# Seven block products for two pairs of each mixer's output projection

## The chip, the cores and the metric

The kernel runs on one core of a Trainium2 chip, as one launch. TensorE multiplies, VectorE and ScalarE work elementwise and empty the accumulators, GpSimd does a little, SyncE issues the loads of the weights. The metric is the device time of the launch in microseconds. The kernel before takes 925.27 us (median of three runs, 924.82 to 926.18).

## The reference, cut to what matters

Two decoder layers over 256 rows of 1024 columns, in float32. Each layer adds half a gated feed-forward network, a mixer, and half a second such network, with a norm ahead of each.

```python
def swiglu(x, w_gate, w_up, w_down):
    return (jax.nn.silu(x @ w_gate) * (x @ w_up)) @ w_down

def ab_mixer(x, w_in, v_norm, w_s, b_s, w_out):          # layer 0
    qa, ka, va, ub, vb = jnp.split(x @ w_in, [512, 1024, 1536, 2048], axis=-1)
    a_out = mixture_of_dilations(heads(qa), heads(ka), heads(va))   # 8 heads of 64
    b_out = gelu(ub) * (causal(w_s) @ rms_norm(gelu(vb), v_norm) + b_s)   # 4 groups of 128
    return jnp.concatenate([a_out, b_out], axis=-1) @ w_out

def c_mixer(x, w_in, w_out):                             # layer 1
    q, k, v = jnp.split(x @ w_in, 3, axis=-1)            # 16 heads of 64, causal softmax
    return from_heads(attention(q, k, v)) @ w_out
...
for layer in range(2):
    h = h + 0.5 * swiglu(rms_norm(h, ffn1_norm[layer]), ...)
    h = h + mixer(rms_norm(h, mix_norm[layer]))
    h = h + 0.5 * swiglu(rms_norm(h, ffn2_norm[layer]), ...)
return rms_norm(h, final_norm)
```

This is a summary of the reference with the shapes put in. With 256 rows the first mixer's three dilations become one masked softmax whose mask holds the logarithm of how many patterns reach a key, and the second mixer's block selection becomes plain causal attention.

## The kernel before

**Products in three parts.** Each float32 operand is split into a high and a low part (`split` L241, `Stream.split_piece` L92: ScalarE copies the high part, VectorE subtracts it from the operand), and each product is three matmuls: high by high, high by low, low by high (`mm3` L236, `rowwise` L377, `colwise` L385, `part` L449).

**The weight stream.** `Stream` (L39) holds every weight of the program in the order of use, in chunks of 1 MB: 512 columns by four k tiles, 256 columns by eight, or, for the second matrix of a stage, a pair of k tiles by 1024 columns. Three raw buffers are loaded ahead (SyncE's queue) and four split buffers are in use or ready. `take` hands out the next chunk, `free` gives one back and `pump` (L117) then issues what has become possible: the next load, the next split. So where `free` stands decides when the following chunks are split. `add_cols` has a number of pieces, in how many parts a chunk is split.

**Two ways to project.** `project` (L401) multiplies the transposed result of a stage (`tiles`, k tiles by two row halves) with the second matrix and adds to the residual `xr`. In the plain way (`part`) a pair of k tiles is 2 k x 2 row halves x 2 column halves, three matmuls each. In the other way (`mixed_part` L412) a pair is seen as two by two blocks times two by two blocks and multiplied by seven products in place of eight. The feed-forward stages do this for the pairs in `MIXED`. It needs sums of blocks on both sides: of the rows (`mix_rows`, L715: four VectorE steps on 128 columns, and a split of the 384 new columns into `seh` and `sel`) and of the weights (`split_mixed` L96: four VectorE steps on 512 columns into `wx`, and their split into `wxh` and `wxl`, one buffer of each). The products of all mixed pairs of a stage gather in seven PSUM banks: `(0,0)`, `(0,1)`, `(1,0)`, 1, 5, 6 and 7. After the last one VectorE and ScalarE join them into the residual (L428 to L445); the lower row half's four steps (`second_rows`) come after the statistics of the upper half. The order of products is sums first for an even pair and own blocks first for an odd one.

**The end of a stage.** The last four k tiles of `project` run for the first row half, whose norm is then formed and transposed under the second row half's matmuls. The second row half's norm (`pend[1].turn`) is transposed within the first block of the next stage. In the feed-forward stages and the second mixer this stands ahead of the last k tile of that block, and the two chunks of the last projection are freed behind it (`behind`, L395). In the first mixer it stands in the middle of its second block, and those two chunks are freed at the end of `project` (L530).

**The first mixer** (`ab_mixer` L844): two blocks of V's 512 columns and two of the gate's 512 columns (each block one row half, 24 matmuls of 512 columns), then four column blocks of u, then q and k for eight heads in eight column blocks, then the projection. `keep_g` (L884) puts the gate's rows through gelu, four sums of squares, a power on GpSimd and a scaling into `vn`. `mixing` (L909) multiplies `vn` with the turned spatial weights for one of four groups, adds a bias, multiplies with u and splits.

**The second mixer** (`c_mixer` L960): two blocks of V's first 512 columns, q and k for heads 0 to 7, two blocks of V's second 512 columns, q and k for heads 8 to 15, then the projection.

**Attention** (`make_attention` L758) runs between these: `scores` of four heads at a time, softmax on VectorE, ScalarE and, in the second mixer, GpSimd; `turn` transposes a head's probabilities; `weighted` forms the weighted sums of V for two heads in one bank and `weighted_two` does so for two pairs in two banks, each split into `mix`. A list of events hung on numbered slots (a slot is one column block of 24 matmuls, a half block, or a k tile of the projection) says when each is traced:

```python
for h, s in enumerate((10, 11, 11, 12, 14, 14, 15, 15)):
    at(s, turn, h)
for h, s in enumerate((8, 8, 8, 8, 12, 12, 12, 12)):
    at(s, scores, h)
for p, s in ((0, 13), (2, 16)):
    at(s, weighted, p)
```

The order of instructions on each engine is fixed when the program is built. A planner there gives each engine, among the instructions whose operands its cost model has ready, the one that was traced first; on the chip each engine runs its list in that order. PSUM has eight banks, handed out by `bank()`.

## Time and profile before

| | |
|---|---|
| median of three runs | 925.27 us |
| profiled execution | 924.85 us |
| its span, first to last instruction | 923.1 us |
| TensorE busy | 915.7 us |
| VectorE busy | 691.9 us |
| ScalarE busy | 538.2 us |
| granted TensorE clock | 0.999 |

A line of the profile names the kernel's line, the engine, the operation, the tile written and the tile read. PE is TensorE, PEld its weight loads, DVE VectorE, ACT ScalarE, POOL GpSimd. A line can be that of a helper: L93 and L94 are every split of a weight, L242 and L243 every other split.

### The profile page before, as it was taken

The page shows a single profiled execution, that of the slowest core. Times are in us where ns is not written, and L with a number is a line of the kernel's source. Part 1 is how long each engine was busy: PE and PEld are TensorE (multiplying, and loading weights), DVE is VectorE, ACT ScalarE, POOL GpSimd, SP SyncE. Part 2 cuts the span into 40 slices and gives each one's busy share as a digit, 9 for nine tenths or more (in the row PEclk, how much of TensorE's full clock was granted, in tenths as well). Part 3 has the DMA queues.
Part 4 walks back from the last instruction along what each step waited for, and adds up shares of the span by engine and source line. Part 5 has one row for each costly group of instructions (what it writes and reads, how often), then busy time and mean ns, then how long its engine had stood idle before and what let it go on. Part 6 is the DMA issues. An engine that isn't in the chain of part 4 may idle for free.

```text
span 923.1 us, 15780 instructions
## 1 busy us (share of the span) xinstructions
PE 915.7 (99%) x6442; PEld 843.2 (91%) x6442; DVE 691.9 (75%) x1044; ACT 538.2 (58%) x842; POOL 35.5 (4%) x53
## 2 busy tenths in 40 slices
PE   9999999999999999999999999999999999999997
PEld 8999998889889999988899999888989799999886
DVE  6886779977657566879876678898656575677797
ACT  6754555585867455546664555556756674555552
POOL 0000000000000000000000000000323100000000
PEclk9999999999999999999999999999999999999999
DMA  9885554757526766536486665473744457665351
GB/s 324 270 275 182 186 180 141 270 175 249 167 91 191 221 185 195 192 131 242 153 274 185 195 207 179 162 243 129 250 150 146 129 167 225 203 204 185 137 182 45
DMA packets 125704, 175.79 MB, mean 190 GB/s; under 512 B 3264, under 2 KB 104768, under 8 KB 125632
## 3 DMA queue, kind: packets, MB, share of 16 engines
q1 hardware_dynamic: 123952, 172.60, 57.5%
q10 hardware_dynamic: 1680, 2.19, 0.8%
q8 instruction: 50, 0.82, 0.4%
q14 instruction: 22, 0.18, 0.1%
HBM read 173.73 MB, written 1.05 MB: 189 GB/s over the span
## 4 chain that ended last, share of the span: by engine, by line
PE 99%; issue 1%; DVE 0%; ACT 0%; POOLq 0%; POOL 0%
PE bank L391 18%; PE bank L393 18%; PE bank L392 18%; PE bank L458 5%; PE bank L462 5%; PE bank L459 5%; PE bank L239 4%; PE bank L237 4%; PE bank L238 4%; PE bank L381 3%; PE bank L383 3%; PE bank L382 3%; PE bank L822 1%; PE bank L782 1%; PE bank L342 1%; PE bank L810 1%
## 5 line engine op out<-in xcount | busy, mean ns | idle before, releaser
L93 ACT ACTIVATE whi<-raw 128x1024 fp32r<-128x1024 f32 (+1 forms) x336 | 329.0, 1029 | 238.8 <-PE bank L392 102.8
L94 DVE TENSOR_TENSOR wlo<-raw,whi 128x1024 fp32r<-128x1024 f32 (+1 forms) x336 | 385.1, 1184 | 84.3 <-ACT whi L93 83.7
L391 PE MATMUL bank<-xTh,whi 128*128 128x256 f32 x1440 | 399.7, 278 | 0.0
L393 PE MATMUL bank<-xTh,wlo 128*128 128x256 f32 x1440 | 398.2, 277 | 0.0
L392 PE MATMUL bank<-xTl,whi 128*128 128x256 f32 x1440 | 398.2, 276 | 0.0
L391 PEld LDWEIGHTS bank<-xTh,whi 128*128 128x128 f32 x1440 | 270.3, 188 | 1.3 <-issue 1.2
L392 PEld LDWEIGHTS bank<-xTl,whi 128*128 128x128 f32 x1440 | 270.8, 188 | 0.1
L393 PEld LDWEIGHTS bank<-xTh,wlo 128*128 128x128 f32 x1440 | 270.5, 188 | 0.0
L674 DVE TENSOR_TENSOR hm<-sil,bank 128x512 f32<-128x512 f32 x38 | 26.1, 687 | 57.2 <-PE bank L393 57.1
L458 PE MATMUL bank<-whi,hTh 128*128 128x512 f32 x152 | 59.8, 393 | 0.0
L459 PE MATMUL bank<-wlo,hTh 128*128 128x512 f32 x152 | 59.2, 390 | 0.0
L242 ACT ACTIVATE hTh<-hm 128x512 fp32r<-128x512 f32 x39 | 24.5, 627 | 50.1 <-DVE hm L719 38.9
L462 PE MATMUL bank<-whi,hTl 128*128 128x512 f32 x152 | 51.4, 389 | 0.0
L94 DVE TENSOR_TENSOR wxl<-wx,wxh 128x1536 fp32r<-128x1536 f32 x24 | 42.1, 1755 | 11.3 <-ACT wxh L93 11.2
L381 PE MATMUL bank<-whi,xTh 128*128 128x512 f32 x112 | 44.4, 397 | 0.0
L383 PE MATMUL bank<-whi,xTl 128*128 128x512 f32 x112 | 43.8, 391 | 0.0
L382 PE MATMUL bank<-wlo,xTh 128*128 128x512 f32 x112 | 43.6, 390 | 0.0
L93 ACT ACTIVATE wxh<-wx 128x1536 fp32r<-128x1536 f32 x24 | 35.5, 1481 | 11.6 <-DVE wx L108 7.7
L249 POOL TENSOR_TENSOR rstd<-ms,half_neg 128x1 f32<-128x1 f32 x14 | 8.1, 582 | 797.2 <-DVE ms L283 792.9
L462 PEld LDWEIGHTS bank<-whi,hTl 128*128 128x128 f32 x152 | 28.5, 188 | 6.0
L459 PEld LDWEIGHTS bank<-wlo,hTh 128*128 128x128 f32 x152 | 28.6, 188 | 5.6
L458 PEld LDWEIGHTS bank<-whi,hTh 128*128 128x128 f32 x152 | 28.6, 188 | 5.5
(165 smaller groups left out, 1150.5 us busy)
## 6 DMA issues: line engine op xcount, KB each, us to landing
raw<-in_ffn_w_down SPq DMA_DIRECT2D x44, 1024.0 KB, 5.0
raw<-in_ffn_w_gate SPq DMA_DIRECT2D x38, 1024.0 KB, 5.5
raw<-in_ffn_w_up SPq DMA_DIRECT2D x38, 1024.0 KB, 5.4
raw<-in_c_w_in SPq DMA_DIRECT2D x12, 1024.0 KB, 5.4
raw<-in_ab_w_in SPq DMA_DIRECT2D x10, 1024.0 KB, 5.4
raw<-in_ffn_w_up SPq DMA_DIRECT2D x12, 512.0 KB, 6.5
raw<-in_ffn_w_gate SPq DMA_DIRECT2D x8, 512.0 KB, 4.0
raw<-in_ab_w_out SPq DMA_DIRECT2D x4, 1024.0 KB, 5.0
```

Of the source, the lines that this page charges most:

```text
L93: self.nc.scalar.activation(hi, raw, AF.Copy)
L94: self.nc.vector.tensor_sub(lo, raw, hi.bitcast(F32))
L237: nc.tensor.matmul(p, sh, mh, start=start, stop=False)
L381: nc.tensor.matmul(p, xh, w[0][:, k, :], start=k0 + k == 0, stop=False)
L382: nc.tensor.matmul(p, xh, w[1][:, k, :], start=False, stop=False)
L383: nc.tensor.matmul(p, xl, w[0][:, k, :], start=False, stop=k0 + k == KD - 1)
L391: nc.tensor.matmul(p, h, xh, start=k == 0, stop=False)
L392: nc.tensor.matmul(p, h, xl, start=False, stop=False)
L393: nc.tensor.matmul(p, l, xh, start=False, stop=k == KD - 1)
L458: nc.tensor.matmul(banks[t, h], sh, w[0][:, kw, cs], start=first, stop=False)
L459: nc.tensor.matmul(banks[t, h], sh, w[1][:, kw, cs], start=False, stop=False)
L462: nc.tensor.matmul(banks[t, h], sl, w[0][:, kw, cs], start=False, stop=last)
```

## The change

- In both mixers two of the four pairs of the output projection are mixed: k tiles 4 to 7 in the first (the gating's four groups), 0 to 3 in the second. `mix_rows` moves out of the feed-forward stage. The mixers get a pool `mq` for the mixed rows and for `wx`, `wxh`, `wxl`.
- The first mixer's gate comes first, V's 512 columns come last, ahead of the projection. The second half's norm is turned in the first block ahead of its last k tile, and the two chunks of the last projection are freed behind that; `project` no longer frees them. Its four chunks for the gate and u are split in four pieces.
- In the second mixer V's second 512 columns come after all q and k. The slots of both mixers are renumbered.
- The weighted sums of two pairs go to the two halves of one bank. Where the pair is mixed, ScalarE copies the bank to SBUF, and the mixed rows and the split are made from the copy.
- The first mixer's gating results are kept for two groups together, for the mixed rows.

```diff
@@ -191,24 +191,23 @@
 
     add_ffn(a["ffn1_w_gate"][0], a["ffn1_w_up"][0], a["ffn1_w_down"][0])
     wab = a["ab_w_in"][0]
-    add_cols(wab, 1024, 512)
-    add_cols(wab, 2048, 512)
-    add_cols(wab, 1536, 256)
-    add_cols(wab, 1792, 256)
+    add_cols(wab, 2048, 512, 4)
+    add_cols(wab, 1536, 256, 4)
+    add_cols(wab, 1792, 256, 4)
     for c in range(2):
         add_cols(wab, c * 256, 256)
         add_cols(wab, 512 + c * 256, 256)
-    add_rows(a["ab_w_out"][0], (4, 6, 0, 2))
+    add_cols(wab, 1024, 512)
+    add_rows(a["ab_w_out"][0], (4, 6, 0, 2), (4, 6))
     add_ffn(a["ffn2_w_gate"][0], a["ffn2_w_up"][0], a["ffn2_w_down"][0])
     add_ffn(a["ffn1_w_gate"][1], a["ffn1_w_up"][1], a["ffn1_w_down"][1])
     wc = a["c_w_in"][0]
     add_cols(wc, 2048, 512, 4)
     for c in range(4):
-        if c == 2:
-            add_cols(wc, 2560, 512)
         add_cols(wc, c * 256, 256, 2 if c else 4)
         add_cols(wc, 1024 + c * 256, 256, 2 if c else 4)
-    add_rows(a["c_w_out"][0], (0, 2, 4, 6))
+    add_cols(wc, 2560, 512)
+    add_rows(a["c_w_out"][0], (0, 2, 4, 6), (0, 2))
     add_ffn(a["ffn2_w_gate"][1], a["ffn2_w_up"][1], a["ffn2_w_down"][1])
 
 
@@ -524,12 +523,21 @@
                     if c == 1 and h == 1 and i == 0:
                         n0.turn_half(1)
                 if c == 1:
-                    add = n1.add(h, banks[1, h], factor)
-                    square = n1.square(h)
+                    n1.add(h, banks[1, h], factor)
+                    n1.square(h)
         n1.root()
-        if nxt == 1:
-            behind(square, add, lambda: st.free(2))
-
+
+
+    def mix_rows(pool, k, hm, e):
+        a11, a21, a12, a22 = (hm[:, i * 128 : (i + 1) * 128] for i in range(4))
+        e = e[:, :384].rearrange("p (j c) -> p j c", j=3)
+        nc.vector.tensor_add(e[:, 0, :], a21, a22)
+        nc.vector.tensor_sub(a21, a11, a21)
+        nc.vector.tensor_sub(e[:, 1, :], e[:, 0, :], a11)
+        nc.vector.tensor_sub(e[:, 2, :], a12, e[:, 1, :])
+        parts = [pool.tile([128, 3, 128], F32R, name=f"{n}{k}") for n in ("seh", "sel")]
+        split(*parts, e)
+        return parts
 
     def heat(n):
 
@@ -712,16 +720,6 @@
             def keep(k, hm):
                 split(hT[0][:, k : k + 2], hT[1][:, k : k + 2], hm.rearrange("p (k t c) -> p k t c", k=2, t=NT))
 
-            def mix_rows(k, hm):
...
             if begin:
                 with tc.tile_pool(name="bp", bufs=1) as bp, tc.manual_schedule():
                     hm = begin(bp, fp, pb)
@@ -748,14 +746,14 @@
                         turn_all()
                 hm = gated(*ps2)
                 if k in MIXED:
-                    mix_rows(k, hm)
+                    mixed[k] = mix_rows(mq, k, hm, fp.tile([128, 512], F32, name="sil", bufs=2))
                 keep(k, hm)
 
             turn_all()
             project(hT, [k + j for k in DOWN for j in range(2)], 4, 0.5, phase + 1, mixed=mixed)
 
 
-    def make_attention(mp, mask_cols, nheads, v, mix, engine):
+    def make_attention(mp, mask_cols, nheads, v, mix, engine, mixed={}, seven=()):
         qs, ks, scs, probs, pts = {}, {}, {}, {}, {}
         mask = mp.tile([128, 384], F32, name="mask")
         nc.scalar.dma_start(mask, a["consts"][:, mask_cols])
@@ -812,8 +810,7 @@
                 pts[p] = mp.tile([128, 2, 384], F32, name="pt", bufs=3)
             nc.scalar.copy(pts[p][:, j, :], tp[:, :384])
 
-        def weighted(p):
-            o = bank()
+        def weighted(p, o):
             pt = pts.pop(p)
...
@@ -821,12 +818,20 @@
                     vs = slice(p * 128 + j * 64, p * 128 + j * 64 + 64)
                     last = nc.tensor.matmul(o[r, S - n : S], v[:, t, vs], pt[:, j, c0 : c0 + n],
                                             start=t == 0, stop=t == 1)
-            split(mix[0][:, p], mix[1][:, p], o[:, :S].rearrange("p (t c) -> p t c", t=NT))
             return last
 
         def weighted_two(p):
-            with tc.issue_after(weighted(p + 1).ins):
-                weighted(p)
+            o = bank()
+            with tc.issue_after(weighted(p + 1, o[:, S:]).ins):
+                weighted(p, o[:, :S])
+            if p in seven:
+                hm = mp.tile([128, 512], F32, name="hm", bufs=2)
+                nc.scalar.copy(hm, o)
+                mixed[p] = mix_rows(st.mix_pool, p, hm, mp.tile([128, 512], F32, name="e"))
+                split(mix[0][:, p : p + 2], mix[1][:, p : p + 2], hm.rearrange("p (k t c) -> p k t c", k=2, t=NT))
+                return
+            for q in (p + 1, p):
+                split(mix[0][:, q], mix[1][:, q], o[:, (q - p) * S : (q - p + 1) * S].rearrange("p (t c) -> p t c", t=NT))
 
         return put_q, put_k, scores, turn, weighted_two
 
@@ -842,7 +847,9 @@
 
 
     def ab_mixer(phase):
-        with tc.tile_pool(name="mp", bufs=1) as mp:
+        with tc.tile_pool(name="mp", bufs=1) as mp, tc.tile_pool(name="mq", bufs=1) as mq:
+            st.mix_pool = mq
+            mixed = {}
             mix = mix_tiles(mp)
             v = v_tile(mp, 512)
             vn = mp.tile([128, NT, 512], F32, name="vn")
@@ -866,17 +873,30 @@
                                         base=0, channel_multiplier=-1)
 
             ws, pb = {}, {}
-
-            def block(t, m, mid=None):
+            ev = {}
+            slot = 0
+
+            def at(s, f, *args):
+                ev.setdefault(s, []).append(lambda: f(*args))
+
+            def step():
+                nonlocal slot
+                run_events(ev, slot)
+                slot += 1
+
+            def block(t, m, mid=None, turned=None):
                 pb[t, m] = bank()
                 for i in range(2):
-                    if i == 1 and mid:
-                        mid()
                     if t == 0:
                         ws[m, i] = st.take()
-                    rowwise(pb[t, m], t, i * 4, ws[m, i], range(4))
+                    if i and turned:
+                        rowwise(pb[t, m], t, 4, ws[m, i], range(3))
+                        turned()
+                    rowwise(pb[t, m], t, i * 4, ws[m, i], range(3, 4) if i and turned else range(4))
                     if t == 1:
                         st.free()
+                    if mid:
+                        mid()
 
             def keep_v(t):
                 nc.vector.tensor_copy(v[:, t, :], pb[t, 0])
@@ -897,31 +917,30 @@
                     nc.vector.scalar_tensor_tensor(vn[:, t, cs], g[:, cs], y[:, q : q + 1], vgain[:, cs],
                                                    op0=ALU.mult, op1=ALU.mult)
 
-            block(0, 0)
-            block(0, 1, pend[1].turn)
-            keep_v(0)
+            block(0, 1, turned=lambda: pend[1].turn((nc.vector, nc.scalar)))
+            behind(*pend[1].turned, lambda: st.free(2))
             keep_g(0)
-            block(1, 0)
             block(1, 1)
-            keep_v(1)
             keep_g(1)
+            twos = []
 
             def mixing(g):
                 p = bank()
                 for t in range(NT):
                     nc.tensor.matmul(p[:, t * 128 : (t + 1) * 128], vn[:, t, g * 128 : (g + 1) * 128],
                                      wsT[:, g, :], start=True, stop=True)
-                tmp = mp.tile([128, NT, 128], F32, name="tmp", bufs=2)
+                if g % 2 == 0:
+                    twos.append(mp.tile([128, 512], F32, name="tmp", bufs=2))
+                two = twos[-1]
+                tmp = two[:, g % 2 * S : g % 2 * S + S].rearrange("p (t c) -> p t c", t=NT)
                 pv = p[:, :S].rearrange("p (t c) -> p t c", t=NT)
                 for t in range(NT):
                     nc.vector.tensor_add(tmp[:, t, :], pv[:, t, :], sbias[:, g * 128 : (g + 1) * 128])
                 nc.vector.tensor_mul(tmp, tmp, uT[:, g, :].rearrange("p (t c) -> p t c", t=NT))
-                split(mix[0][:, 4 + g], mix[1][:, 4 + g], tmp)
-
-            ev = {}
-
-            def at(s, f, *args):
-                ev.setdefault(s, []).append(lambda: f(*args))
+                if g % 2:
+                    mixed[3 + g] = mix_rows(mq, 3 + g, two, mp.tile([128, 512], F32, name="e"))
+                    split(mix[0][:, 3 + g : 5 + g], mix[1][:, 3 + g : 5 + g],
+                          two.rearrange("p (k t c) -> p k t c", k=2, t=NT))
 
             turn_spatial()
             for i, s in enumerate((2, 4, 5, 6)):
@@ -930,18 +949,16 @@
                 at(s, turn, h)
             for h, s in enumerate((8, 8, 8, 8, 12, 12, 12, 12)):
                 at(s, scores, h)
-            for p, s in ((0, 13), (2, 16)):
+            for p, s in ((0, 17), (2, 19)):
                 at(s, weighted, p)
 
-            slot = 0
             for c in range(2):
                 w = st.take()
                 for j in range(2):
                     p = bank()
                     colwise(p[:, :S], w, j)
                     nc.scalar.activation(uT[:, 2 * c + j, :], p[:, :S], AF.Gelu_apprx_tanh)
-                    run_events(ev, slot)
-                    slot += 1
+                    step()
                 st.free()
             for c in range(2):
                 for put in (put_q, put_k):
@@ -950,18 +967,23 @@
                         p = bank()
                         colwise(p[:, :S], w, j)
                         put(2 * c + j, p)
-                        run_events(ev, slot)
-                        slot += 1
+                        step()
                     st.free()
-            project(mix, [4, 5, 6, 7, 0, 1, 3, 2], 4, 1.0, phase + 1, lambda i: run_events(ev, 12 + i))
+            for t in range(NT):
+                block(t, 0, step)
+                keep_v(t)
+            project(mix, [4, 5, 6, 7, 0, 1, 3, 2], 4, 1.0, phase + 1, lambda i: step(), mixed)
             assert not ev
 
 
     def c_mixer(phase):
-        with tc.tile_pool(name="mp", bufs=1) as mp:
+        with tc.tile_pool(name="mp", bufs=1) as mp, tc.tile_pool(name="mq", bufs=1) as mq:
+            st.mix_pool = mq
+            mixed = {}
             mix = mix_tiles(mp)
             v = v_tile(mp, D)
-            put_q, put_k, scores, turn, weighted = make_attention(mp, slice(384, 768), 16, v, mix, nc.gpsimd)
+            put_q, put_k, scores, turn, weighted = make_attention(mp, slice(384, 768), 16, v, mix, nc.gpsimd,
+                                                                  mixed, (0, 2))
             ws, pb = {}, {}
 
             def block(t, m, mid=None, turned=None):
@@ -991,20 +1013,17 @@
                 run_events(ev, slot)
                 slot += 1
 
-            for h, s in enumerate((6, 7, 7, 8, 10, 11, 12, 12, 18, 18, 19, 19, 22, 22, 23, 23)):
+            for h, s in enumerate((6, 7, 7, 8, 10, 11, 11, 12, 14, 15, 15, 16, 18, 18, 19, 19)):
                 at(s, turn, h)
-            for h, s in enumerate((4, 4, 4, 4, 8, 8, 8, 8, 16, 16, 16, 16, 20, 20, 20, 20)):
+            for h, s in enumerate((4, 4, 4, 4, 8, 8, 8, 8, 12, 12, 12, 12, 16, 16, 16, 16)):
                 at(s, scores, h)
-            for p, s in ((0, 10), (2, 14), (4, 21), (6, 24)):
+            for p, s in ((0, 10), (2, 14), (4, 21), (6, 23)):
                 at(s, weighted, p)
 
             block(0, 0, turned=lambda: pend[1].turn((nc.vector, nc.scalar)))
             behind(*pend[1].turned, lambda: st.free(2))
             block(1, 0)
             for c in range(4):
-                if c == 2:
-                    block(0, 1, step)
-                    block(1, 1, step)
                 for put in (put_q, put_k):
                     w = st.take()
                     for j in range(2):
@@ -1013,7 +1032,9 @@
                         put(2 * c + j, p)
                         step()
                     st.free()
-            project(mix, [0, 1, 2, 3, 4, 5, 7, 6], 4, 1.0, phase + 1, lambda i: step())
+            block(0, 1, step)
+            block(1, 1, step)
+            project(mix, [0, 1, 2, 3, 4, 5, 7, 6], 4, 1.0, phase + 1, lambda i: step(), mixed)
             assert not ev, ev.keys()
 
 
```

More of the change, by code (lines that the diff above doesn't have):

```diff
@@ L713, in keep @@
                 split(hT[0][:, k : k + 2], hT[1][:, k : k + 2], hm.rearrange("p (k t c) -> p k t c", k=2, t=NT))
-            def mix_rows(k, hm):
-                a11, a21, a12, a22 = (hm[:, i * 128 : (i + 1) * 128] for i in range(4))
-                e = fp.tile([128, 512], F32, name="sil", bufs=2)[:, :384].rearrange("p (j c) -> p j c", j=3)
-                nc.vector.tensor_add(e[:, 0, :], a21, a22)
-                nc.vector.tensor_sub(a21, a11, a21)
-                nc.vector.tensor_sub(e[:, 1, :], e[:, 0, :], a11)
-                nc.vector.tensor_sub(e[:, 2, :], a12, e[:, 1, :])
-                mixed[k] = [mq.tile([128, 3, 128], F32R, name=f"{n}{k}") for n in ("seh", "sel")]
-                split(*mixed[k], e)
             if begin:
```

## The prediction

> **What bounds the kernel now.** I read the page's busy times and its chain of waits first, then the projection's matmuls in the groups by line and in the timeline, then busy times by stage.
>
> ```profile
> span 923.1 us, 15780 instructions
> PE 915.7 (99%) x6442; PEld 843.2 (91%) x6442; DVE 691.9 (75%) x1044; ACT 538.2 (58%) x842; POOL 35.5 (4%) x53
> PE 99%; issue 1%; DVE 0%; ACT 0%; POOLq 0%; POOL 0%
> ```
>
> The chain that ended last is matmuls almost alone. Between the opening and the closing norm TensorE never stands still, so a removed matmul is worth what it occupies, unless its removal, or what pays for it, makes TensorE wait.
>
> A matmul's own duration is not that price, because matmuls overlap:
>
> ```profile
> L458 PE MATMUL bank<-whi,mixh 128*128 128x512 f32 x64 | 26.3, 411 | 0.0
> L459 PE MATMUL bank<-wlo,mixh 128*128 128x512 f32 x64 | 25.1, 391 | 0.0
> L462 PE MATMUL bank<-whi,mixl 128*128 128x512 f32 x64 | 22.6, 394 | 0.0
> ```
>
> ```profile
> 268.67 0.39 PE L458 MATMUL bank<-whi,mixh 128*128 128x512 f32 x1
> 268.90 0.39 PE L459 MATMUL bank<-wlo,mixh 128*128 128x512 f32 x1
> 269.12 0.39 PE L462 MATMUL bank<-whi,mixl 128*128 128x512 f32 x1
> 269.35 0.39 PE L458 MATMUL bank<-whi,mixh 128*128 128x512 f32 x1
> ```
>
> The two mixers hold 3 x 64 = 192 projection matmuls. One lasts 0.39 us but the next starts 0.227 us later (268.67 to 269.35 is three). The price is 0.227.
>
> **What is removed.** A plain pair of k tiles takes 2 k x 2 row halves x 2 column halves x 3 = 24 matmuls; seven products take 7 x 3 = 21. Two pairs in each of two mixers: 4 x 3 = 12 matmuls, 12 x 0.227 = 2.72 us. Every other matmul and transpose stays and only moves.
>
> [...]
>
> **What is added** falls on VectorE and ScalarE, and has rows in the feed-forward stages, which do the same already:
>
> ```profile
> L103 DVE TENSOR_TENSOR wx<-raw 128x512 f32<-128x512 f32 x24 | 16.5, 689 | 0.4
> L94 DVE TENSOR_TENSOR wxl<-wx,wxh 128x1536 fp32r<-128x1536 f32 x24 | 42.1, 1755 | 11.3 <-ACT wxh L93 11.2
> L93 ACT ACTIVATE wxh<-wx 128x1536 fp32r<-128x1536 f32 x24 | 35.5, 1481 | 11.6 <-DVE wx L108 7.7 <-PE bank L239 3.9
> L718 DVE TENSOR_TENSOR sil<-hm 128x128 f32<-128x128 f32 x24 | 7.0, 292 | 0.8
> L243 DVE TENSOR_TENSOR sel<-sil,seh 128x384 fp32r<-128x384 f32 x24 | 13.2, 552 | 0.0
> L242 ACT ACTIVATE seh<-sil 128x384 fp32r<-128x384 f32 x24 | 12.4, 517 | 1.5 <-DVE sil L721 1.5
> L437 DVE TENSOR_TENSOR wx<-bank,wx 128x512 f32<-128x512 f32 x4 | 2.8, 688 | 0.7 <-ACT wx L436 0.7
> L436 ACT COPY wx<-bank 128x512 f32<-128x512 f32 x4 | 2.3, 574 | 2.7 <-DVE x L433 2.7
> L94 DVE TENSOR_TENSOR wlo<-raw,whi 128x1024 fp32r<-128x1024 f32 x312 | 369.7, 1222 | 81.6 <-ACT whi L93 81.0
> L94 DVE TENSOR_TENSOR wlo<-raw,whi 128x512 fp32r<-128x512 f32 x24 | 15.6, 687 | 2.7 <-ACT whi L93 2.7
> ```
>
> Per mixer, on VectorE: two weight chunks with four sums and one more split, 2 x (4 x 0.69 + 1.755) = 9.0; two pairs of mixed rows, 2 x (4 x 0.29 + 0.55) = 3.4; the eight steps that join the products, 8 x 0.69 = 5.5. Together 17.9 us; in the first mixer some 1.2 more, since four chunks are split in quarters (16 x 0.69 for 8 x 1.22). On ScalarE 2 x (1.48 + 0.52) + 0.57 = 4.6, and in the second mixer two copies of a shared bank, 0.57 each. Does it hide?
>
> ```profile
> 126.00:183.00 57.00, 57.00 (x263) 47.38 (x261) 51.51 (x58) 32.48 (x38) 0.55 (x1) 1.00 0.60 203
> 183.00:279.00 96.00, 96.00 (x630) 84.33 (x629) 62.13 (x138) 70.00 (x161) 4.34 (x6) 1.00 0.51 164
> 636.00:744.00 108.00, 108.00 (x762) 94.94 (x761) 68.56 (x163) 69.75 (x161) 24.95 (x30) 1.00 0.49 161
> ```
>
> Columns: window, length, then busy time of TensorE, its loads, VectorE, ScalarE and GpSimd. The first row is a feed-forward projection with six such pairs: VectorE at 51.5 of 57 (90%), TensorE never idle. The mixers (second and third row) would go from 62 to 81 of some 95 us (86%) and from 69 to 87 of 107 (81%), ScalarE to some 76 of 95. So TensorE's work hides it, at nothing; without that cover it would be 18 us a mixer. The granted clock, 1.00 in each row, stays.
>
> **What is moved.** The projection's first pairs now need seven banks of eight; V's second block moves ahead of the projection as filler, so scores and transposes are through before. Only the weighted sums fall into it, and one bank a visit is what is left for them. The visits into TensorE's stream stay as many in the first mixer and are two fewer in the second, about 0.1 us each way per visit: a gain of up to 0.3.
>
> In the first mixer one block less runs ahead of the second half's turn, whose `free(2)` (two loads, two splits) now comes after the turn, as already in the other stages:
>
> ```profile
> 634.87 0.39 PE L383 MATMUL bank<-whi,xTl 128*128 128x512 f32 x1
> 635.10 1.03 PE L342 MATMUL bank<-ident,xn 128*128 128x128 f32 x8
> 635.52 2.18 ACT L352 ACTIVATE xTh<-bank,gT 128x128 fp32r<-128x128 f32 x8 [0.81 <-PE bank L342]
> 635.89 0.48 PE L381 MATMUL bank<-whi,xTh 128*128 128x512 f32 x1
> 636.21 0.39 PE L382 MATMUL bank<-wlo,xTh 128*128 128x512 f32 x1
> ```
>
> There TensorE goes from matmul to transposes with 0.23 us and resumes with 0.32 for 0.23: 0.09 us and no wait. I take zero; from -0.1 to +0.5, the latter if the gate's table load and statistics slip between.
>
> The gate is less sure. Its statistics now stand right behind that turn, with V's 10.9 us of cover (48 matmuls x 0.227) gone:
>
> ```profile
> 183.71 0.40 PE L381 MATMUL bank<-whi,xTh 128*128 128x512 f32 x1
> 195.54 1.28 ACT L886 ACT_TABLE_LOAD   x1
> 206.69 0.60 ACT L886 ACTIVATE gv<-bank 128x512 f32<-128x512 f32 x1 [0.77 <-ACT whi L93]
> 207.32 0.31 ACT L889 ACTIVATE vn<-gv 128x128 f32<-128x128 f32 x1
> 208.92 2.01 ACT L93 ACTIVATE whi<-raw 128x1024 fp32r<-128x1024 f32 x2 [0.90 <-DMA raw<-in_ab_w_in]
> 213.59 1.14 DVE L897 SCALAR_TENSOR_TENSOR vn<-gv,rsg,vgain 128x128 f32<-128x128 f32 x4 [1.14 <-POOL rsg L249]
> 215.06 0.60 PE L912 MATMUL bank<-wsT,vn 128*128 128x128 f32 x4
> ```
>
> From the second half's gate (206.69) to the mixing (215.06) TensorE has 8.4 us of other work, and the operand was there about 1.1 us early (213.59 plus a quarter of 1.14), although two of the four statistics stood behind two splits that had waited 0.9 us for a load; they ended some 0.6 us after those, at 211.5, and the operand 2.4 us later.
>
> Afterwards TensorE reaches the mixing near 215.06 - 10.9 = 204.2. The turn's transposes come 21 matmuls into the block that begins at 183.71, at 188.5, and ScalarE is through with the evictions 2.6 us later (635.10 to 637.70 above), near 191.1. Then come two chunks' splits (2 x 2.01), the first half's table load and statistics (1.28 + 0.6 + 4 x 0.31 = 3.1), and either the second half's statistics first (1.9) or two more splits before them (4.0). With 2.4 us behind, the operand is ready near 202.5 or near 206.5: between no wait and 2.3 us, 3.2 with a load's 0.9. What hides it is TensorE's 8.4 us of column blocks, which it has as before; what would be late next is the mixing alone, whose result only the projection wants. The rows show the planner dealing out instructions by what it expects to be ready (splits between statistics), so I take 0.2, near the lower end.
>
> **The sum.** 2.72 + 0.2 - 0.2 = 2.7 us off the profiled execution, 924.85 (its span 923.1 and 1.75 around it), gives 922.1; the runs' median is 925.27, 0.4 above it, so 922.6.
>
> **The rivals.** *The mixing waits.* As just priced, up to 3.2 us; for it the 0.9 us by which a load came later than its place in ScalarE's order supposed, against it that the planner may send TensorE to another column block first: 923.4 to 925.8, middle 924.5.
>
> *GpSimd late in the second mixer.* It scales the probabilities, and VectorE's new two-operand work falls beside it.
>
> ```profile
> L802 POOL TENSOR_SCALAR pr<-pr,rl x28: 601/922/1982, 659.5 to 718.3; 128x128 f32<-128x128 f32 x14, 128x256 f32<-128x256 f32 x14
> 715.51 1.51 POOL L802 TENSOR_SCALAR pr<-pr,rl 128x128 f32<-128x128 f32 x2 [6.76 <-DVE rl L795]
> 717.17 1.52 PE L822 MATMUL bank<-pt,vt 128*64 128x256 f32 x16
> 721.47 0.82 PE L810 MATMUL bank<-ident,pr 128*128 128x128 f32 x6
> ```
>
> The same step, in its two widths, lasts 601 to 1982 ns, so at most 1.4 us more at a time; the last visit has 721.47 - 717.02 = 4.4 us to spare. Three or four such delays use that up; six would hold TensorE some 4 us: up to 926.6, middle 924.6. [...]
>
> *Slower: the second chunk's split is late.* Both chunks of a mixer use one pair of `wxh` and `wxl`, so the second is split only when the first's sums have left TensorE. Then TensorE has two sets of own products (24 x 0.227 = 5.4) and a weighted visit (1.5, the row at 717.17) while 1.48 on ScalarE and 1.755 on VectorE must end: 3.7 us to spare. It decides once more than 3.7 us of other VectorE work is queued ahead. Two plain chunks (4 x 1.22 = 4.9) and the second's four raw sums (2.8) are 7.7, which holds TensorE 4.0 us in each mixer: 922.6 + 8 = 930.6. With half of that the gain is gone and 926.6 results. For it: VectorE in order and fuller than before. Against: six pairs in the first window above have the same 5.4 us and no wait.
>
> **How the numbers follow.** A run of this kernel tells 0.2% (1.85 us) from no change. The forecast, all but 0.9 us of the gain kept, gets 0.60, its own range 921.8 to 923.4 (lower end: lowest run 924.82 less 2.72 and 0.3). The mixing's wait 0.20 and GpSimd 0.07: 0.27 within 0.2%. The late second split 0.13, all on slower. The range goes from 921.8 to 926.0, just past where the mixing's wait ends, and leaves out that last rival.
>
> **What would show it.** Right: 180 projection matmuls where 192 were, TensorE's starts 0.227 us apart in the sevens, no wait named on TensorE, VectorE near 86% and 81% in the mixers, each mixer 1.3 us shorter. Wrong: a gap ahead of L912's successor near 204 us (the mixing), ahead of the transposes of late heads (GpSimd), or ahead of the products with `wxh` of a mixer's second pair (the late split); or a mixer that is not shorter though nothing waits.

## The result: slower by 0.67%, and the profile after

The changed kernel takes 931.68 us in the median (929.98 to 933.05); the kernel before, on the same chip, 925.14 (924.82 to 926.18). The ratio is 1.0067, its 95% interval 1.0054 to 1.0080. The forecast was 922.6, faster, in a range of 921.8 to 926.0: the sign is wrong and the range too short.

The page of the changed kernel, its busy times, the chain that ended last, and the granted clock in 40 slices:

```profile
PE 917.3 (98%) x6430; PEld 842.8 (90%) x6430; DVE 722.5 (78%) x1105; ACT 546.2 (59%) x857; POOL 40.6 (4%) x53
PE 91%; DVE 3%; ACT 3%; issue 1%; DMA 1%; POOL 0%; SPq 0%; POOLq 0%
...
PEclk9999999998999999999999999999999999999999
```

TensorE has 6430 matmuls where it had 6442: the twelve are gone. The chain of waits, before 99% TensorE, now passes through VectorE, ScalarE and a DMA for 7%; and one slice has a lower clock. The profiled execution took 933.05 us; it is the slowest of the six, 1.4 above the median, so what is read from its trace below is the long case.

The two largest waits of TensorE, with us in total, times and the longest:

```profile
PE bank L930 <- DVE vn L917: 2.8, 1, 2.8
PE bank L457 <- ACT mixh L241: 2.6, 2, 1.6
```

Before, the one wait named on TensorE was at the start. To find the stages, I take as landmarks the transposes of the residual halves (line 342 before, 341 after), the first half's turn at the head of a stage. Rows of before and then of after, start and length in us:

```profile
181.44 0.60 PE L342 MATMUL bank<-ident,xn 128*128 128x128 f32 x4
272.07 0.60 PE L342 MATMUL bank<-ident,xn 128*128 128x128 f32 x4
...
628.05 0.60 PE L342 MATMUL bank<-ident,xn 128*128 128x128 f32 x4
737.15 0.60 PE L342 MATMUL bank<-ident,xn 128*128 128x128 f32 x4
```

```profile
182.46 0.60 PE L341 MATMUL bank<-ident,xn 128*128 128x128 f32 x4
280.73 0.66 PE L341 MATMUL bank<-ident,xn 128*128 128x128 f32 x4
...
636.75 0.60 PE L341 MATMUL bank<-ident,xn 128*128 128x128 f32 x4
745.42 0.62 PE L341 MATMUL bank<-ident,xn 128*128 128x128 f32 x4
```

The first mixer went from 90.6 to 98.3 us, 7.6 longer. The second went from 109.1 to 108.7: 0.4 shorter, where 1.3 was foreseen. The feed-forward stages between them are equal (355.98 and 356.02). Another 1.0 us was lost ahead of the first mixer (181.44 and 182.46), all of it within the first 11 us of the launch, whose code is not changed; 0.5 of it is a wait for a weight's split at 9.6 us. The profiles of the other changed kernels reach this landmark at 181.3 to 182.3, so I take it for the chance of one execution. The rest of the loss lies in the first mixer, most of it in three places.

**The mixing.** TensorE, then ScalarE and VectorE of the changed kernel ahead of 210 us, start and length in us; brackets hold the idle time before the row and what ended it:

```profile
205.21 0.38 PE L930 MATMUL bank<-wsT,vn 128*128 128x128 f32 x2
...
206.13 0.28 PE L390 MATMUL bank<-xTh,whi 128*128 128x256 f32 x1
206.25 0.28 PE L391 MATMUL bank<-xTl,whi 128*128 128x256 f32 x1
209.38 0.80 PE L930 MATMUL bank<-wsT,vn 128*128 128x128 f32 x2 [2.85 <-DVE vn L917]
210.19 0.41 PE L390 MATMUL bank<-xTh,whi 128*128 128x256 f32 x1
210.40 0.41 PE L391 MATMUL bank<-xTl,whi 128*128 128x256 f32 x1
```

```profile
194.28 4.27 ACT L93 ACTIVATE whi<-raw 128x512 fp32r<-128x512 f32 x8
...
199.62 2.00 ACT L93 ACTIVATE whi<-raw 128x1024 fp32r<-128x1024 f32 x2
...
202.78 2.01 ACT L93 ACTIVATE whi<-raw 128x1024 fp32r<-128x1024 f32 x2 [0.89 <-DMA raw<-in_ab_w_in]
204.69 0.57 ACT L906 ACTIVATE gv<-bank 128x512 f32<-128x512 f32 x1
```

```profile
208.97 1.14 DVE L917 SCALAR_TENSOR_TENSOR vn<-gv,rsg,vgain 128x128 f32<-128x128 f32 x4 [1.13 <-POOL rsg L248]
```

The first row half of the mixing (205.21) found its operand; the second (209.38) did not. The last matmul into the bank of the second row half's gate had ended at 196.7 (196.34 and 0.40), but ScalarE came to that gate at 204.69, 8.0 us later: it stands behind twelve splits in its list, the last two of which also waited 0.89 us for a load; from there to the operand at 208.97 are another 4.3 us. TensorE is done with what it has at 206.5 and stands.

**The clock behind it.** Stretches from that wait on: window and length, busy time of TensorE, its loads, VectorE, ScalarE and GpSimd with their counts, granted clock, DMA share, GB/s:

```profile
208.70:208.80 0.10, 0.00 (x0) 0.00 (x0) 0.00 (x0) 0.10 (x1) 0.10 (x1) 0.50 1.06 379
212.00:216.00 4.00, 4.00 (x23) 4.00 (x23) 2.28 (x6) 2.27 (x3) 0.00 (x0) 0.56 0.71 231
215.50:215.60 0.10, 0.10 (x3) 0.10 (x2) 0.10 (x1) 0.10 (x1) 0.00 (x0) 0.92 1.00 389
216.00:220.00 4.00, 4.00 (x38) 4.00 (x37) 3.19 (x9) 0.96 (x3) 0.00 (x0) 1.00 0.60 188
```

From 212 to 216 TensorE is busy throughout and does 23 matmuls where the next window has 38. Matmuls of 256 columns start 0.21 us apart (210.19, 210.40) in place of 0.12 (206.13, 206.25). The clock is 1.00 up to 208.6, 0.50 from 208.7 to 215.5, and 1.00 again behind that; the 0.56 is an average over the return. From 210.19 to 215.31 are 24 steps from start to start in 5.1 us, which at 0.114 apart (216.00 to 217.02) would be 2.7: 2.4 us lost there. Counted to the third mixing, against an execution with the same wait and no dip (last section), the dip cost 2.9, after a wait of 2.85.

**The head of the projection.** TensorE and ScalarE from 264.7 to 271.3 us:

```profile
264.73 0.50 PE L236 MATMUL bank<-whi,seh 128*128 128x512 f32 x1
...
265.85 1.52 PE L819 MATMUL bank<-pt,vt 128*64 128x256 f32 x16
...
267.96 1.52 PE L819 MATMUL bank<-pt,vt 128*64 128x256 f32 x16
271.08 0.50 PE L457 MATMUL bank<-whi,mixh 128*128 128x512 f32 x1 [1.60 <-ACT mixh L241]
```

```profile
266.77 0.86 ACT L811 COPY pt<-bank 128x384 f32<-128x384 f32 x2
...
268.74 2.01 ACT L93 ACTIVATE whi<-raw 128x1024 fp32r<-128x1024 f32 x2
270.63 0.67 ACT L241 ACTIVATE mixh<-bank 128x256 fp32r<-128x256 f32 x2
```

One of the seven products of both pairs (`whi` by `seh`, in a bank of its own) is put off to the very end, and both visits of weighted sums come behind one another only there, at 265.85 and 267.96. The copies of the last two heads' turned probabilities come only when the first visit is under way (266.77). The splits of the mixed tiles are then the last thing, and the plain pairs wait for them. The second mixer has the same picture with a wait of 1.04. In the first mixer the two waits and the dip are 7.3 us; with the 1.4 that six products were to save, 9.0 are to be explained, so 1.7 are left open here.

### The profile page after: what moved, and what is told of

Read it like the earlier page. It is cut to its first block, busy times and chain, and to the rows that moved or that the text cites. A ratio compares the mean times of both kernels' runs of the same rounds, so it can differ in the third digit from the quotient of the medians.

```text
span 931.3 us, 15840 instructions
## 1 busy us (share of the span) xinstructions
PE 917.3 (98%) x6430; PEld 842.8 (90%) x6430; DVE 722.5 (78%) x1105; ACT 546.2 (59%) x857; POOL 40.6 (4%) x53
## 4 chain that ended last, share of the span: by engine, by line
PE 91%; DVE 3%; ACT 3%; issue 1%; DMA 1%; POOL 0%; SPq 0%; POOLq 0%
PE bank L390 17%; PE bank L392 17%; PE bank L391 17%; PE bank L236 5%; PE bank L238 5%; PE bank L237 5%; PE bank L457 5%; PE bank L458 4%; PE bank L461 4%; PE bank L380 2%; PE bank L381 2%; PE bank L382 2%; DVE wlo L94 2%; ACT whi L93 1%; PE bank L341 1%
## 5 line engine op out<-in xcount | busy, mean ns | idle before, releaser
L94 DVE TENSOR_TENSOR wxl<-wx,wxh 128x1536 fp32r<-128x1536 f32 x28 | 49.1, 1754 | 15.3 <-ACT wxh L93 15.2
L93 ACT ACTIVATE wxh<-wx 128x1536 fp32r<-128x1536 f32 x28 | 41.5, 1481 | 15.1 <-DVE wx L108 10.5
```

The costliest lines, as they stand in the source:

```text
L93: self.nc.scalar.activation(hi, raw, AF.Copy)
L94: self.nc.vector.tensor_sub(lo, raw, hi.bitcast(F32))
```

## The experiments

All edits are to the changed kernel. Times in us; before is 925.05 to 925.23 in the median beside them.

| kernel | median | range | ratio to before, 95% |
|---|---|---|---|
| changed | 931.68 | 929.98 to 933.05 | 1.0054 to 1.0080 |
| mixings later | 927.88 | 927.68 to 928.39 | 1.0017 to 1.0038 |
| four `pt` buffers | 928.54 | 927.99 to 928.97 | 1.0021 to 1.0046 |
| both edits | 925.27 | 924.70 to 925.74 | 0.9992 to 1.0010 |
| more matmuls ahead of the mixing | 930.62 | 929.84 to 931.01 | 1.0044 to 1.0069 |
| second mixer alone | 923.64 | 923.24 to 924.11 | 0.9977 to 0.9994 |
| both edits, first projection plain | 923.20 | 922.39 to 925.08 | 0.9971 to 0.9989 |
| the same again | 922.52 | 922.22 to 923.78 | 0.9962 to 0.9983 |
| both edits, probabilities on GpSimd | 928.08 | 927.13 to 931.06 | 1.0028 to 1.0059 |
| both edits, chunk given back later | 926.59 | 925.86 to 927.97 | 1.0008 to 1.0026 |
| both edits, one pair in the first mixer | 923.27 | 922.63 to 924.07 | 0.9971 to 0.9989 |
| first projection plain, two banks a visit | 923.90 | 923.29 to 925.80 | 0.9977 to 0.9995 |

### The mixings later

```diff
-            for i, s in enumerate((2, 4, 5, 6)):
+            for i, s in enumerate((4, 5, 6, 7)):
                 at(s, mixing, i)
```

> The changed kernel with the gate's four mixings attached to slots 4, 5, 6, 7 in place of 2, 4, 5, 6: nothing else is edited, and the first mixing then stands two projections of u later in TensorE's stream, behind its operand. Theory W+C (the wait of 3.0 us at 206.25 and a lowered clock for some 5.5 us behind it): 931.7 less 3.0 less 0.9 to 2.7, so 926 to 928, and no granted clock below 0.95 between 200 and 220 us. Theory W (the wait alone; the clock is unrelated): about 928.7, and a low clock somewhere still. Rival B (the wait only moves: other work at this place is late anyway, for instance the planner's later mixings or the splits): no change within 0.5 us of 931.7.

927.88, 3.8 less, in the range of wait and clock together. The wait is gone and the clock is 1.00 in the windows from 200 to 220 us. The operand is 0.8 us earlier than above, as is the whole stage (181.62 against 182.46); TensorE, which now comes to it at 209.80, finds it there:

```profile
208.13 1.14 DVE L917 SCALAR_TENSOR_TENSOR vn<-gv,rsg,vgain 128x128 f32<-128x128 f32 x4 [1.13 <-POOL rsg L248]
```

In the profiled executions the first mixer is 4.5 us shorter (93.7 against 98.3). Part of the gain came back as a wait that was not there, ahead of the second scores:

```profile
PE bank L780 <- DVE k L770: 1.2, 1, 1.2
```

### Four buffers of turned probabilities

```diff
-                pts[p] = mp.tile([128, 2, 384], F32, name="pt", bufs=3)
+                pts[p] = mp.tile([128, 2, 384], F32, name="pt", bufs=4)
```

> The changed kernel with four buffers of turned probabilities (pt) in place of three, nothing else. Theory P (with three buffers the fourth pair's transposes hold two banks until the first pair's weighted sums have run; seven products and two banks are nine of eight, so one product of each seven-product pair and the weighted sums are put off, and the last splits of mixed tiles come late): the gaps ahead of the weighted sums and ahead of the plain pairs (1.3 us near 271, 0.75 near 735.8) go, the products run in order, 931.7 less 2 to 4, so 927.7 to 929.7. Rival S (the one shared bank of a visit, or VectorE and ScalarE loaded by the mixed rows, sets these gaps): no change within 0.5 us. The wait ahead of the mixing and the low clock near 210 stay under both.

928.54, 3.1 less, in the middle of theory P. The products now run in order, the visits come between them at 259.92 and 266.29, and of the 2.6 us ahead of the plain pairs 0.3 is left:

```profile
265.39 0.50 PE L457 MATMUL bank<-whi,mixh 128*128 128x512 f32 x1 [0.34 <-ACT mixh L241]
```

So three buffers for four pairs were the cause. By the kernel's text, the last pair's transposes could not leave their two banks until a visit had given a buffer free, and seven products and two banks do not fit in eight. The profiled executions differ by 2.0 us in this (1.1 in the second mixer; 0.9 in the first, after the 2.9 of the dip is taken off, which only the changed kernel has there).

### Both edits

> Both edits: mixings at slots 4 to 7 and four pt buffers. If W+C and P are the whole of it, what is left is the removal of twelve products of 0.227 us: 925.1 less 2.7 is 922.4, with 0.3 to 1.5 for the turn in the first block and the start, so 922.4 to 924, faster than before. If VectorE's and ScalarE's added work is the loss after all (rival S, B), 928 or more.

925.27: neither theory. It is 6.4 below the changed kernel (the two edits alone sum to 6.9), and level with before, so some 2.7 us of the gain are still missing. With the mixings late, where no clock dipped, the fourth buffer was worth 2.6 (927.88 to 925.27). The second mixer has its share of the gain in full: 107.4 us between its landmarks (630.37 and 737.80) against 109.1. The first is 92.9 against 90.6. What waits there, and VectorE's rows at that place:

```profile
PE bank L780 <- DVE k L770: 1.5, 1, 1.5
...
PE bank L808 <- ACT pr L798: 0.4, 1, 0.4
PE bank L457 <- ACT mixh L241: 0.3, 1, 0.3
```

```profile
234.66 1.76 DVE L94 TENSOR_TENSOR wxl<-wx,wxh 128x1536 fp32r<-128x1536 f32 x1 [1.48 <-ACT wxh L93]
236.34 2.35 DVE L94 TENSOR_TENSOR wlo<-raw,whi 128x1024 fp32r<-128x1024 f32 x2
238.61 0.41 DVE L770 COPY k<-bank 128x256 f32<-128x256 f32 x1
```

The copy of the last k, for which TensorE stands, is behind the first seven-product chunk's splits, 4.1 us on VectorE. It came last, but not alone: the weight load of the same scores names ScalarE's copies of turned probabilities, which stand behind the same chunk's splits there:

```profile
PEld bank L780 <- ACT pt L811: 1.9, 1, 1.9
```

The same window of before and of this kernel (VectorE is the third busy time; the blocks in it are not the same, since their order changed):

```profile
236.00:242.00 6.00, 6.00 (x54) 6.00 (x53) 2.18 (x13) 6.00 (x22) 0.00 (x0) 1.00 0.48 161
```

```profile
236.00:242.00 6.00, 4.52 (x31) 3.18 (x30) 6.00 (x9) 4.26 (x8) 0.00 (x0) 1.00 0.38 110
```

### More matmuls ahead of the mixing

```diff
                 p = bank()
+                for _ in range(17 if g == 0 else 0):
+                    nc.tensor.matmul(p[:, :128], vn[:, 0, :128], wsT[:, 0, :], start=True, stop=True)
                 for t in range(NT):
```

> The changed kernel with 17 more matmuls of the first mixing's first half (128 by 128, result thrown away, some 0.22 us each) ahead of the first mixing, so that TensorE is busy through the 3 us in which it waited; 17 products that compute nothing new, no other edit. The mixing's operand comes at the same time, and three other products that ran before the wait now run after it (1.0 us more). Theory C (the low clock after the wait is the wait's doing): no granted clock under 0.95 near 210, 931.7 plus 1.0 less 0.9 to 2.7, so 930.0 to 931.8, and in the profiled runs the stretch from the mixing's operand to the end of u's products 2.7 us shorter for the same work. Theory N (the clock dips for another reason): the dip stays and the time is 932.7 or more.

930.62, theory C. TensorE does useless work through what was the wait and takes up its own work hardly earlier (the first matmul behind the mixing is 27.2 us behind the stage's first turn, 27.4 with the wait). The whole is 1.1 us shorter, although three products moved behind the filler; in the profiled executions the first mixer is 2.2 us shorter (96.1 against 98.3). The clock stays in the trace, and the mean clock is 0.998 or 0.999 in all five executions, where the changed kernel had 0.995 to 0.998:

```profile
208.00:216.00 8.00, 7.99 (x71) 7.80 (x70) 6.93 (x13) 3.09 (x6) 0.61 (x1) 1.00 0.88 305
```

### The second mixer alone

The first mixer, its order of weights and the step behind the first norm are those of before; the second mixer is changed, with four `pt` buffers.

> The first mixer as before (plain projection, V's block where it was, two banks a visit); the second mixer changed, with four pt buffers. Theory L (in the second mixer, VectorE and ScalarE hide the added work; the first mixer's loss is its own): the 109.1 us between the second mixer's turns becomes 107.4, as with both edits, so 925.1 less 1.7 is 923.4, 922.9 to 923.9, faster than before. Rival G (the second mixer's gain in the run with both edits came from somewhere else, or is eaten by stages behind it): 924.5 or more.

923.64, theory L: faster than before by 0.15%, interval 0.06 to 0.23%. The second mixer is 107.3 us between the same landmarks (627.87 to 735.18) against 109.1, 1.8 shorter, and no wait but the one at the start is named. The added work is there and hidden: from 636 us to the next stage's turn, VectorE is at 83.0 of 106 us, before 68.6 of 108:

```profile
636.00:742.00 106.00, 106.00 (x753) 93.23 (x752) 83.03 (x189) 74.30 (x165) 29.02 (x30) 1.00 0.50 164
```

### Both edits, the first projection plain

```diff
-    add_rows(a["ab_w_out"][0], (4, 6, 0, 2), (4, 6))
+    add_rows(a["ab_w_out"][0], (4, 6, 0, 2))
...
-                    mixed[3 + g] = mix_rows(mq, 3 + g, two, mp.tile([128, 512], F32, name="e"))
```

> Both edits (mixings at slots 4 to 7, four pt buffers), but the first mixer's projection plain again: 96 products in place of 90 there, no weight sums, no sums of mixed rows, no joining steps; the order of blocks stays changed. Theory V (the first mixer's remaining loss, 2.3 us against before where 1.4 less was due, is the added weight sums and splits on VectorE and ScalarE: 1.5 us ahead of the scores of the second half of the pairs, 0.4 and 0.5 ahead of transposes, 0.3 ahead of the plain pairs): these waits go, the first mixer is within 0.5 us of before, and the time is 925.1 less 1.7 plus 0 to 0.5, 923.4 to 923.9. Theory R (the new order of the blocks, V last, makes these waits by itself): the waits stay, 1.4 us is added for the six products, 926.0 or more.

923.20, theory V, and 0.2 better than it said. Six products more, and yet 2.1 us faster: the waits for k, for the transposes and for the mixed tiles are all gone. The first mixer, in its new order, takes 90.15 us (181.32 to 271.47), 0.5 less than before. So the new order costs nothing by itself; what cost time came with the seven products, their added work or the seven banks that they hold, which no run here parts:

```profile
183.00:278.00 95.00, 95.00 (x627) 83.41 (x626) 62.34 (x141) 68.87 (x162) 5.28 (x6) 1.00 0.50 166
```

```profile
183.00:281.00 98.00, 95.56 (x623) 82.18 (x622) 76.95 (x169) 72.87 (x167) 5.29 (x6) 1.00 0.48 161
```

The first row is this kernel, the second the one with both edits: 14.6 us more on VectorE, and TensorE busy for 95.6 of 98.

### Two attempts to make room: GpSimd, and a later free

```diff
-            ... = make_attention(mp, slice(0, 384), 8, v, mix, nc.scalar)
+            ... = make_attention(mp, slice(0, 384), 8, v, mix, nc.gpsimd)
```

> Both edits, and in the first mixer the probabilities are scaled by GpSimd, which is idle there, in place of ScalarE (16 steps of some 0.38 us; the second mixer does so already). If ScalarE's queue is what makes the scores' chain and the splits late (ScalarE 6.0 of 6.0 us busy from 230 to 236), the waits shrink by 1 to 2.5 us: 922.8 to 924.3. If VectorE's own work is the limit, or GpSimd's slower steps lengthen the chain from scores to transposes, no gain: 925 to 926.

928.08, 2.8 slower than with both edits, worse than either case. ScalarE is relieved, and a longer chain takes its place; GpSimd's eight steps fill 11.5 us without a break, 1.4 each, where ScalarE took 0.4 (four in 1.50 us with both edits):

```profile
PE bank L808 <- POOL pr L800: 4.6, 5, 3.0
```

```profile
229.50 11.48 POOL L800 TENSOR_SCALAR pr<-pr,rl 128x128 f32<-128x128 f32 x8 [21.55 <-DVE rl L793]
```

```diff
-                    st.free()
+                    if c == 0:
+                        st.free()
+                if c == 1:
+                    st.free(2)
```

> Both edits, and in the first mixer the chunk of the second q is given back together with that of the second k, so that the sums and splits of the first seven-product chunk are traced behind the copies of k and not ahead of them. If the wait for k (1.5 us near 238) is only an order in VectorE's queue, it goes and nothing takes its place: 923.5 to 924.3. If the work itself is too much for the stretch up to the projection, the wait moves to the first seven products (their sums and splits, some 13 us on VectorE for two chunks, come up to 6 us later): 925 or more, with a wait on the split of wx or wxh at the projection's head.

926.59, 1.3 slower. The wait for k went, as an order in a queue would, but the work did not: it now stands in VectorE's list ahead of the softmax of the last scores (235.62 to 242.54), whose probabilities come late. I had expected that wait at the products' splits; it is at the transposes.

```profile
PE bank L808 <- ACT pr L798: 3.2, 2, 2.6
```

### One pair as seven products in the first mixer

The second mixed chunk of the first mixer (rows 6, 7) is plain, with the sums of its mixed rows left out.

> The version with both edits, but in the first mixer only one pair of k tiles (4, 5) as seven products, the other three pairs plain: half of the added weight sums, splits and sums of mixed rows there, the joining steps in full. Theory V by degree (the second chunk's work is what overfills VectorE and ScalarE ahead of the projection; a single chunk still fits): no wait over 0.2 us, three products fewer than with a plain first projection, 923.2 less 0.7 is 922.5. Rival Q (the wait for k comes from the first chunk alone, since its splits of 1.8 and 2.4 us stand ahead of the copies of k): the wait of about 1.5 us stays, 923.2 less 0.7 plus 1.5 is 924.0 or more.

923.27, between the two: the wait for k is half as long, so neither theory holds as put.

```profile
PE bank L780 <- DVE k L770: 0.7, 1, 0.7
```

On the same chip the plain first projection took 922.52. Three products fewer (0.68 us) came out 0.75 slower: the wait of 0.7 undoes the removal, 0.3 more lies in the first mixer (90.5 us between its landmarks against 90.15), where the eight joining steps stay in full (that they are the cause was not tried). Of the other 0.4, 0.2 lies at the start of the launch in the profiled executions (181.55 against 181.31), and the rest I can't place.

### Two banks a visit

```diff
             o = bank()
+            o2 = bank()[:, :S] if seven and p not in seven else o[:, :S]
             with tc.issue_after(weighted(p + 1, o[:, S:]).ins):
-                weighted(p, o[:, :S])
+                weighted(p, o2)
```

> The version with a plain first projection (mixings at slots 4 to 7, four pt buffers, second mixer with its two pairs as seven products), but the second mixer's visits of pairs 4, 5 and 6, 7 take two banks each again, as before the change. Theory K (with seven banks held by the products, one bank a visit is what fits; a visit with two has to break up around the products): the visits come in two halves, each 0.1 to 0.2 us dearer, and the last mixed tiles come later, 923.2 plus 0.3 to 1.5. Rival O (the shared bank is not needed, the visits find two banks): 923.2 within 0.3.

> The same kernel as the one with a plain first projection, once more, beside the other two of this set: 923.2, 922.8 to 923.7, faster than before by 0.2 percent; were it the chance of one chip, 924.5 or more.

923.90 against 922.52: theory K. The two visits break into four, and the second mixer is 108.2 us (627.80 to 735.97) against 107.5 (627.43 to 734.92). No wait is named there, so these 0.7 us are in the stops themselves; of the other 0.7 of the medians, 0.4 lies at the start of the launch in the profiled executions (181.67 against 181.31), and the rest I can't place. The first of the four, with eight matmuls where a whole visit has sixteen:

```profile
717.62 0.87 PE L819 MATMUL bank<-pt,vt 128*64 128x256 f32 x8
```

The repeated kernel, 922.52, is the fastest here, 0.28% below before (0.17 to 0.38%). It is 0.3 below the range that I had given it and 0.7 below the same kernel's 923.20, so a comparison between sets of runs is no finer than that.

## Why the prediction was wrong

**What held.** Twelve matmuls went, at 0.227 us: the second mixer alone shows it, 1.8 us where 1.36 and up to 0.3 for the visits were counted. The turn in the first block cost nothing that a row shows. Neither GpSimd nor the late second split held TensorE up in the changed kernel: no wait on `wxh`, `wxl` or the second mixer's probabilities over 0.3 us is named. GpSimd's steps there, of both widths, took 599 to 2705 ns where they had taken 601 to 1982, with the same median of 922; no run shows that VectorE's work beside them is what lengthens them. The size of the added VectorE work was put too high, 17.9 us a mixer and 1.2 more in the first, where 14.5 and 14.8 were measured. The lengths of the rows do add up as counted (74.6 to 92.5 in the second mixer), but rows of a full queue overlap: with both edits, VectorE's steps of 0.68 at 240.68, 241.28 and 241.88 are 0.60 apart. A VectorE row's length (0.68 for a step of 0.60) is no more its price than a matmul's is (0.39 for 0.227).

**"... so I take 0.2, near the lower end."** The first step that failed is this term. The wait was 2.85, and the upper bound of 3.2 had its mechanism right: more splits ahead of the second half's gate, and the load's 0.9. It was even short: TensorE reached the mixing at 205.21, near the place foreseen, and the operand let it go on at 209.38, 4.2 us later, of which other work filled 1.3. Two gelus of u among ScalarE's splits (0.37 each, at 201.52 and 205.17) and the splits in quarters (4.27 for 4.02) were not in the working. I chose the lower end because the planner hands out by what it expects to be ready. It held back the mixing's second half by eight matmuls (starts from 205.34 to 206.25) and no more; behind that TensorE stood for 2.85 us, with whole column blocks left to do behind the mixing in its list.

**"The granted clock, 1.00 in each row, stays."** It held where TensorE had no long wait: 0.998 or 0.999 in every execution of the changed kernels whose longest wait was 1.6 us or less. In the changed kernel's own profiled execution, within a wait of 2.85 us, it fell to 0.50 for 6.8 us, at a cost of 2.9, which doubles the wait's price; the other executions, at mean clocks of 0.996 to 0.998 for its 0.995, took 1.2 to 3.1 us less. The rival "the mixing waits" had no clock in it: it priced this place at up to 3.2, and wait and clock together came to 3.8 in the medians, already less a new wait of 1.2.

**"... so scores and transposes are through before. Only the weighted sums fall into it, and one bank a visit is what is left for them."** This named the resource (seven banks of eight) and left out a second one, the three `pt` buffers. I counted the transposes as done when they were issued; they hold their bank until the copy, and that copy waits for a buffer that only a visit gives free. It cost 2.6 to 3.1 us by the four buffers (927.88 to 925.27, and 931.68 to 928.54). That one bank a visit is what fits was right, and is worth 0.7 us in the second mixer.

**"So TensorE's work hides it, at nothing."** It does in the second mixer and not in the first. The share foreseen over the mixer, 86%, was an average (measured: 77.0 of 98 us, 79%): between 236 and 242 us VectorE was full, with k's copy behind 4.1 us of splits. With both faults mended, the seven products made the first mixer 2.1 to 2.75 us slower than the plain projection (925.27 against 923.20 and 922.52): 3.4 to 4.1 us were paid there for 1.36 saved, of which the rows name 2.2 as waits. The other 1.2 to 1.9 no row names; whether they come from the load or from the banks held was not tried. The rival for the slower side had this mechanism (VectorE in order, fuller than before) at the wrong place: the products with `wxh` had the time to spare that I had counted, the small copies on which the next step hangs had none.

As a sum: 925.1, less 2.7 for the products, less 0.4 for the rest of the second mixer's gain and 0.5 for the first mixer's new order, plus 3.4 to 4.1 for the first mixer's load, is 924.9 to 925.6, where 925.27 was measured; the buffers and the mixing with its clock add 6.4 to 931.7. The 3.4 to 4.1 are read from these same runs, so the sum closes by its making; it shows how large each part is, not that one could have been foreseen.

## What to carry to other kernels

Count a bank, or any buffer, as taken until its reader has run, and then ask what that reader waits for: here a second resource (`pt`) closed the circle, at 2.6 to 3.1 us. Share of busy time over a stage doesn't tell whether added work hides (VectorE's 79% of the first mixer held six full microseconds, and a wait of 1.5); look at the fullest few microseconds and at the small instruction there that another engine waits for. A wait of TensorE can cost more than its length, as the traced 2.85 us did with the 2.9 of the dip behind it, so a bound for it should carry the clock.

## What the runs showed of the hardware

The lower clock does not follow from every such wait. The four `pt` buffers' kernel had the same wait (2.85 us ahead of the mixing) and in its profiled execution no dip:

```profile
208.00:216.00 8.00, 6.82 (x60) 6.82 (x60) 7.18 (x14) 3.48 (x6) 0.75 (x1) 1.00 0.89 305
```

Its second row half of the first mixing and its third mixing (the first fence), and the third mixing of the changed kernel:

```profile
209.19 0.49 PE L930 MATMUL bank<-wsT,vn 128*128 128x128 f32 x2 [2.85 <-DVE vn L917]
214.07 0.60 PE L930 MATMUL bank<-wsT,vn 128*128 128x128 f32 x4
```

```profile
217.13 0.60 PE L930 MATMUL bank<-wsT,vn 128*128 128x128 f32 x4
```

From the end of the wait to the third mixing are 4.88 us here and 7.75 with the dip (209.38 to 217.13), for the same matmuls: 2.9 us is its price.

That execution took 927.99 at a mean clock of 0.999; the other four of this kernel took 928.26 to 928.97 at 0.996 or 0.997; what dips those had, and at what price, their times alone don't show. The kernel with GpSimd (longest wait 3.0) ran from 927.13 at 0.999 to 931.06 at 0.994, the one with the chunk given back later (longest wait 2.6) was at 0.997 to 0.999. The changed kernel itself was at 0.995 to 0.998. Every changed kernel whose longest wait was 1.6 us or less was at 0.998 or 0.999 in every execution. So among the executions of the four kernels with a longest wait of 2.6 to 3 us in their traces, some had a lower mean clock and others not, and the times spread with it; the dip itself is traced in one. It is not the only way to a lower mean clock: one of 69 executions of the kernel before beside the experiments was at 0.997 too (928.72). In the one traced dip TensorE had stood for 2.2 us when the clock fell (206.53 to 208.7) and stood 2.85 in all. The clock was at 0.50 for 6.8 us (208.7 to 215.5), and back 6.1 us after TensorE's work had begun again (209.38). Why one wait of 2.85 us is followed by a dip and another is not, no run here shows.
